# Convolution operands scaled by 1/rms from the third chunk on, and four taps moved from TensorE to VectorE, in a two-layer decoder trunk

## The chip, the core and the metric

The kernel runs on one core of a Trainium2 chip. Five engines work side by side, each through its own queue of instructions and in that queue's order: TensorE (PE: products), VectorE (DVE), ScalarE (ACT), GpSimd (POOL) and SyncE (SP, which here issues most of the DMAs). They wait for one another by semaphores. SBUF is the on-chip memory of 128 partitions; PSUM holds what TensorE writes. The metric is the time of one execution on the device in microseconds (us); of several runs the median is given.

## What is computed

Two decoder layers over 512 tokens of 1024 channels. Layer 0 begins with a causal Conformer convolution, the only part that the change touches:

```python
u = rms_norm(h, conv_norm_g)                       # u = h * rsqrt(mean(h*h)) * g
a = u @ w_pw1 + b_pw1                              # 1024 -> 2048
u = a[..., :1024] * sigmoid(a[..., 1024:])
u = conv(u, dw_w) + dw_b                           # 31 taps per channel, causal
u = silu(layer_norm(u, ln_g, ln_b))
h = h + u @ w_pw2 + b_pw2
```

Behind it come a SwiGLU feed-forward part, a gated per-layer embedding p, and layer 1 with differential attention. All data is float32.

## The kernel before

Activations lie with channels on partitions: `h[c]` is chunk c (0 to 7) of 128 channels by 512 tokens. A float32 product is made of three products in a rounded format: each operand is split into a rounded half (`hi`, a ScalarE cast) and a remainder (`lo`, a subtraction), and `mm3` (L165) adds lo x hi, hi x hi and hi x lo. A weight tile of 128x1024 goes through `weight` (L148): a DMA on SP into one of two raw buffers (`wraw`), a ScalarE cast into `whi`, a subtraction into `wlo` on VectorE or GpSimd. The next DMA into a raw buffer waits until both have read it, and SP's later DMAs stand behind it in the queue.

**The first matrix, w_pw1.** For chunk c there are a gate half and a value half, each 8 x 3 products into a PSUM tile `mm` (four of them exist). The operands are h times g alone (`Norm.split`, L211); the factor 1/rms of each token isn't known yet when TensorE begins. It comes from the token-major copy of x: ScalarE squares, VectorE and GpSimd make the inverse root, `spread` (L274) writes it to all partitions of a PSUM tile (`tp`), and `rows` (L246) copies it to SBUF as `rb`. When a half is done, VectorE multiplies it by `rb` (L612 for the gate, L618 for the value); ScalarE takes the sigmoid (L613); VectorE adds the value's bias and multiplies by the gate (L624 or L632; the "forming" instruction).

**The taps.** Chunks 1, 3, 5 and 6 (`PHASED`) are convolved on TensorE: the formed chunk goes to device memory and comes back ordered by token phases (`phased_in`, tile `C1`), TensorE multiplies by banded matrices that are loaded from `diag` (L462, into PSUM `sc` or `mm`), ScalarE copies the result (L470) and stores it (`po`, a DMA that ScalarE issues), SP loads it back in token order, and VectorE adds the bias and the mean row (`shift`, L482). Chunks 0, 2, 4 and 7 are convolved tap by tap (`other_taps`, L493): VectorE adds taps into PSUM (L518); 10, 11, 11 and 7 of the taps (`POOL_TAPS`) are products of ScalarE (L508) that GpSimd adds up (L509); and eight of chunk 7 (`PE_TAPS`) are products of TensorE with diagonal matrices (L412, in full float32). `BETWEEN` and `BEHIND` say at which chunk's matrix products the taps of an earlier chunk are issued.

**Statistics.** Once y of chunk 0 is there, its column mean (L558) gives `shrow`, a row that is added to all later chunks before their sums are taken; the first VectorE tap of chunks 2, 4 and 7 reads it (L541, L522). `moments` (L564) squares each y on ScalarE, and GpSimd adds sums and squares (L575, L571). For chunk 7 the order on VectorE is written out by hand: first tap, two taps, `shift` of chunk 5, 11 taps, `shift` of chunk 6, two taps, two additions. TensorE then fills its time with products for the embedding p (`factor`), transposes the sums (L671), and after the inverse root the rows with w_pw2 follow.

**Order.** Where no order is written by hand (`manual_schedule`, `issue_after`), a list scheduler places each instruction in its engine's queue. `pfeatures` (L357) loads p for layer 0 into the same two raw buffers and splits it, the remainder on GpSimd (L362).

Of the kernel before, what the change touches and what calls it, by code (L numbers as in the profile page):

```python
# [13 lines left out]
F32R = mybir.dt.float32r  # L14
# [6 lines left out]
P = 128  # L21
# [28 lines left out]
WARM = 9  # L50
ALONE = (7,)
CUTS = 2


PE_TAPS = (0, 0, 0, 0, 0, 0, 0, 8)
POOL_TAPS = (10, 0, 11, 0, 11, 0, 0, 7)


# [33 lines left out]
def trunk(ctx, tc, xT, xtok, pT, wts, diag, dww, vec, rel, onehot, lamv, out):  # L92
# [97 lines left out]
    def both(t):  # L190
        return t[:, 0], t[:, 1]
# [12 lines left out]
    class Norm:  # L204


        def __init__(self, g, acc_engine=None):
            self.g, self.u = g, []
            self.eng = acc_engine or G

        def split(self, c):  # L211
            hi, lo = both(sb([P, 2, S], f"A{c}", 1, F32R))
            split_scaled(h[c], col(self.g, c), hi, lo)
            self.u.append((hi, lo))

# [30 lines left out]
        def rows(self):  # L246

            r = sb([P, S], "rb", 1)
            last_rows[0] = A.copy(r, spread(self.dg))
            return r  # L250

    last_v = [None]
    last_pow = [None]
# [32 lines left out]
    raws = [sb([P, 1024], "wraw", 2) for _ in range(2)] + [sb([P, 1024], f"B{i}", 1) for i in (2, 3)]
    first = [tuple(sb([P, 1024], t, 4, F32R) for t in ("whi", "wlo")) for _ in range(4)]
    pieces = slice(0, HT), slice(HT, S), slice(S, 1024)
# [46 lines left out]

    with tc.manual_schedule(engines={V.engine, A.engine}):
        first_split(0, pieces[0])
        norm.split(0)
        first_split(1, pieces[0])
        norm.split(1)  # L340
        first_split(0, pieces[1])
        first_split(1, pieces[1])
        norm.split(2)
        norm.split(3)
        first_split(0, pieces[2])
        first_split(1, pieces[2])
        for c in range(4, NC):
            norm.split(c)
        first_split(2, whole)
        square(0)  # L350
        square(1)
        first_split(3, whole)
        square(2)
        square(3)
        norm.factors_of(sums_x)

    def pfeatures(layer, parts):  # L357
        for k, (hi, lo) in enumerate(parts):
            raw = sb([P, 1024], "wraw", 2)[:, :S]
            nc.sync.dma_start(raw, pT[layer, :, k * S : (k + 1) * S])  # L360
            A.copy(hi, raw)
            (G if layer == 0 else V).tensor_tensor(lo, raw, f(hi), ALU.subtract)  # L362
        return parts

    last_product = [None]
# [15 lines left out]
    accs = {}  # L381
    last_tap = [None]
    outs = {}
    shifts = []
    last_part = [None]
    outer = []
# [8 lines left out]
    def wt(c, j):  # L395
        return dwt[:, c * KW + j : c * KW + j + 1]
# [70 lines left out]
    def phased_out(c):  # L467

        o = big()
        A.copy(o, accs[c])  # L470
        d = dram.tile([P, S], F32, tag=f"po{c}", name=f"po{c}")
        outs[c] = nc.scalar.dma_start(d, o)
        both_ = sb([P, 2, S], f"B{c}", 1)
        for g in range(NPH):
            nc.sync.dma_start(
                both_[g * FG : (g + 1) * FG, 1].rearrange("p (r n) -> p r n", r=NPH),
                bass.AP(d.tensor, d.offset + g * P, [[S, FG], [FG * S, NPH], [1, P]]),
            )
        tok = "p (n r) -> p n r"

        def shift():
            V.scalar_tensor_tensor(  # L482
                both_[:, 0].rearrange(tok, r=NPH), both_[:, 1].rearrange("p (r n) -> p n r", r=NPH), col("dw_b", c),
                shrow.rearrange(tok, r=NPH), ALU.add, ALU.add,
            )
            y[c] = both_[:, 0]

        if c < NC - 3:
            shift()
        else:  # L490
            shifts.append(shift)

    def other_taps(c, behind=None):  # L493
        if c in PHASED:
            return phased_out(c)
        up, acc = ups[c], accs[c]
        alone = c in ALONE
        tap = lambda j: up[:, j : j + S]
        a, b = PE_TAPS[c], PE_TAPS[c] + POOL_TAPS[c]
        pacc = wk()  # L500
        for j in range(a, b):
            if j == a:
                with tc.issue_after(outs[5].ins) if alone else nullcontext():
                    A.activation(pacc, tap(j), AF.Identity, scale=wt(c, j), bias=col("dw_b", c))
            else:
                pr = sb([P, S], f"C{2 + j % 2}", 2)
                with tc.issue_after(outs[6 if j == b - 1 else 5].ins) if alone else nullcontext():
                    A.activation(pr, tap(j), AF.Copy, scale=wt(c, j))  # L508
                last_part[0] = G.tensor_tensor(pacc, pacc, pr, ALU.add)  # L509
        yc = sb([P, 2, S], f"B{c}", 1)  # L510
        if c == 0:
            sums["acc"] = yc[:, 1]
        yc = yc[:, 0]
        sum_ = sc() if alone else acc

        def taps(js):
            for j in js:
                V.scalar_tensor_tensor(sum_, tap(j), wt(c, j), sum_, ALU.mult, ALU.add)  # L518

        if alone:  # L520
            with tc.manual_schedule(engines={V.engine}):
                V.scalar_tensor_tensor(sum_, tap(b), wt(c, b), shrow, ALU.mult, ALU.add)  # L522
                taps(range(b + 1, b + 3))
                shifts[0]()
                moments(NC - 3)
                taps(range(b + 3, KW - 2))
                shifts[1]()
                outer.append(weight(eng=G, after=(last_part[0], None)))
                taps(range(KW - 2, KW))
                moments(NC - 2)  # L530
                outer.append(weight(eng=G, after=(last_sq[0], None)))
                V.tensor_tensor(yc, sum_, pacc, ALU.add)
                V.tensor_tensor(yc, acc, yc, ALU.add)
                y[c] = yc
                moments(c)
            return
        with tc.issue_after(behind.ins) if behind else nullcontext():
            if c == 0:
                V.tensor_scalar(sum_, tap(b), wt(c, b), None, ALU.mult)
            else:  # L540
                V.scalar_tensor_tensor(sum_, tap(b), wt(c, b), shrow, ALU.mult, ALU.add)  # L541
        taps(range(b + 1, KW))
        V.tensor_tensor(yc, sum_, pacc, ALU.add)
        y[c] = yc

# [8 lines left out]
    def moments(c):  # L554
# [21 lines left out]
        if c == NC - 2:  # L576
            add_square()

    for c in range(NC):
        wa, wg = pairs[c]  # L580
        if c == 0:
# [14 lines left out]
                    if k == 0:  # L596
                        rb = norm.rows()
        if 0 < c < NC - 1:
            late = ((first_gate, last_rows[0]),) * 2 if c == 1 else ((None, None),) * 2
            pairs.append(tuple(weight(after=i) for i in late)[::-1])  # L600
            pair_loads.append(loaded[0])
        if c == 1:
            ph = pfeatures(0, [(sb([P, S], t, 2, F32R), sb([P, S], t, 2, F32R)) for t in ("wth", "wtl")])
        if c > 0:
            pg = half(wg) if c > 1 else g1
            for k in BETWEEN[c]:
                pe_taps(k)
            pa = half(wa) if c > 1 else a1
            for k in BEHIND[c]:
                pe_taps(k)  # L610
        tg, ta = big(), big()
        V.tensor_tensor(tg, pg, rb, ALU.mult)  # L612
        gated = A.activation(tg, tg, AF.Sigmoid, bias=col("b_pw1", 8 + c))  # L613
        if c == NC - 1:

            with tc.issue_after(gated.ins):
                A.activation(powers[:, 24:32], vt[:, :8], AF.Silu)
        scaled = V.tensor_tensor(ta, pa, rb, ALU.mult)  # L618
        if c == 0:
            first_gate = scaled  # L620
        if c in PHASED:
            up = big()
            phases, tok = "p (r n) -> p n r", "p (n r) -> p n r"
            formed = V.scalar_tensor_tensor(  # L624
                up.rearrange(phases, r=NPH), ta.rearrange(tok, r=NPH), col("b_pw1", c),
                tg.rearrange(tok, r=NPH), ALU.add, ALU.mult,
            )
            phased_in(c, up)
        else:
            up = ups[c] = sb([P, S + PAD], "C0", 2)  # L630
            G.memset(up[:, :PAD], 0.0)
            V.scalar_tensor_tensor(up[:, PAD:], ta, col("b_pw1", c), tg, ALU.add, ALU.mult)  # L632
        for k in BETWEEN[c] + BEHIND[c]:
            other_taps(k, formed if k == 4 else None)
        if c == 1:
# [947 lines left out]
```

## Time and profile before

| | |
|---|---|
| time, median of 3 runs | 1236.92 us (1236.35 to 1238.66) |
| the profiled execution, own time | 1238.28 us |
| its span, first to last instruction | 1236.3 us |
| TensorE busy | 1224.5 us (99%) |
| VectorE, ScalarE, GpSimd busy | 880.1, 625.1, 474.3 us |
| mean granted clock of TensorE | 0.999 |

Rows of the profile name the source line (L518), the engine, the operation, the tiles written and read, and a count (x11). In a timeline a row begins with its start and its length in us; in groups, busy time and the mean of one in ns stand behind the bar, then the idle time of the engine ahead of it and what ended that. In the rows by stage the engines are in the order PE, PEld (weight loads of TensorE), DVE, ACT, POOL, and then the granted clock, the share of DMA and GB/s. The chain of waits follows the work that ended last back through what released it. TensorE's products overlap: one takes 0.39 us, the next begins sooner.

### The profile page before, as it was taken

To read this page: it belongs to the slowest core of one execution; us is meant where nothing else is said; L and a number is where in the kernel's file an instruction comes from. 1 tells how busy PE (TensorE), PEld (TensorE's weight loads), DVE (VectorE), ACT (ScalarE), POOL (GpSimd) and SP (SyncE) were. 2 spreads that over 40 slices of the span, in tenths; PEclk is the share of its full clock that TensorE was granted. 3 is DMA by queue.
4 is the path that set the end of the run, shared out by engine and by line. 5 is a ranking of instruction groups with operands and counts; after the bars stand their busy time and mean duration, and the time that the engine had idled before them with its cause. 6 is when DMAs were issued, how large, how long until landed. Compare 5 with 4: busy or idle time off the path is not lost.

```text
span 1236.3 us, 18296 instructions
## 1 busy us (share of the span) xinstructions
PE 1224.5 (99%) x7011; PEld 1072.4 (87%) x7011; DVE 880.1 (71%) x1251; ACT 625.1 (51%) x1099; POOL 474.3 (38%) x355
## 2 busy tenths in 40 slices
PE   9999999999999999999999999999999999999998
PEld 7888688888998899888788888888889998999887
DVE  5889866975895479547767776747966884588545
ACT  6563464533553255434657777735534552455432
POOL 0594813024670464133436636131026640562220
PEclk9999999999999999999999999999999999999999
DMA  8664323333333322334423321142243333233331
GB/s 328 224 209 144 106 68 110 93 106 119 93 96 119 102 86 73 116 105 153 125 85 105 99 86 53 56 150 85 90 132 90 100 120 108 80 103 86 105 99 69
DMA packets 50019, 138.44 MB, mean 112 GB/s; under 512 B 5731, under 2 KB 10851, under 8 KB 49932
## 3 DMA queue, kind: packets, MB, share of 16 engines
q1 hardware_dynamic: 47664, 133.71, 35.1%
q10 hardware_dynamic: 2268, 3.57, 1.0%
q8 instruction: 55, 0.90, 0.3%
q14 instruction: 32, 0.26, 0.1%
HBM read 130.94 MB, written 6.31 MB: 111 GB/s over the span
## 4 chain that ended last, share of the span: by engine, by line
PE 84%; DVE 7%; DMA 4%; issue 3%; ACT 1%; POOL 1%; SPq 0%; ACTq 0%; DVEq 0%; POOLq 0%
PE mm L167 26%; PE mm L168 26%; PE mm L169 26%; DMA wraw<-in_wts 2%; DVE sc L518 2%; PE mm L1282 1%; DVE wlo L162 1%; PE sc L1242 1%; PE tp L1269 1%; PE sc L1239 1%; PE sc L462 1%; DMA B<-po 1%; DVE wlo L863 1%; POOL wk L509 0%; PE tp L1190 0%
## 5 line engine op out<-in xcount | busy, mean ns | idle before, releaser
L160 ACT CAST whi<-wraw 128x1024 fp32r<-128x1024 f32 (+1 forms) x139 | 141.3, 1026 | 233.4 <-PE mm L169 108.5
L167 PE MATMUL mm<-A,wlo 128*128 128x512 f32 (+1 forms) x540 | 209.7, 388 | 0.7 <-ACT A L201 0.6
L162 DVE TENSOR_TENSOR wlo<-wraw,whi 128x1024 fp32r<-128x1024 f32 (+1 forms) x132 | 167.6, 1276 | 59.7 <-ACT whi L160 59.2
L168 PE MATMUL mm<-A,whi 128*128 128x512 f32 (+1 forms) x540 | 208.6, 386 | 0.0
L169 PE MATMUL mm<-A,whi 128*128 128x512 f32 (+1 forms) x540 | 206.6, 387 | 0.1
L167 PE MATMUL mm<-B,wlo 128*128 128x512 f32 x352 | 137.0, 389 | 0.0
L168 PE MATMUL mm<-B,whi 128*128 128x512 f32 x352 | 137.0, 389 | 0.0
L224 POOL TENSOR_TENSOR acc<-acc,wk 128x512 f32<-128x512 f32 x35 | 60.9, 1741 | 195.3 <-ACT wk L223 170.8
L169 PE MATMUL mm<-B,whi 128*128 128x512 f32 x352 | 135.6, 389 | 0.0
L168 PE MATMUL mm<-C,whi 128*128 128x256 f32 x448 | 126.8, 283 | 0.0
L169 PE MATMUL mm<-C,whi 128*128 128x256 f32 x448 | 126.8, 283 | 0.0
L167 PE MATMUL mm<-C,wlo 128*128 128x256 f32 x448 | 126.8, 283 | 0.0
L863 DVE TENSOR_TENSOR wlo<-A,whi 128x1024 fp32r<-128x1024 f32 x60 | 106.7, 1789 | 20.0 <-ACT whi L862 20.0
L167 PEld LDWEIGHTS mm<-A,wlo 128*128 128x128 f32 x540 | 101.5, 188 | 22.0 <-ACT A L201 1.0
L169 PEld LDWEIGHTS mm<-A,whi 128*128 128x128 f32 x540 | 101.5, 188 | 21.3 <-DVE A L202 0.8
L168 PEld LDWEIGHTS mm<-A,whi 128*128 128x128 f32 x540 | 101.6, 188 | 20.1
L862 ACT CAST whi<-A 128x1024 fp32r<-128x1024 f32 x60 | 63.1, 1051 | 55.7 <-PE mm L169 44.7
L872 POOL TENSOR_TENSOR A<-wraw 128x512 f32<-128x512 f32 x16 | 24.7, 1541 | 170.8 <-DMA wraw<-in_wts 155.3
L168 PEld LDWEIGHTS mm<-C,whi 128*128 128x128 f32 x448 | 86.0, 192 | 0.2
L167 PEld LDWEIGHTS mm<-C,wlo 128*128 128x128 f32 x448 | 86.0, 192 | 0.2
L169 PEld LDWEIGHTS mm<-C,whi 128*128 128x128 f32 x448 | 86.0, 192 | 0.0
L872 POOL TENSOR_TENSOR A<-A 128x512 f32<-128x512 f32 x16 | 24.7, 1546 | 159.0 <-DMA A<-in_wts 156.5
(354 smaller groups left out, 3083.5 us busy)
## 6 DMA issues: line engine op xcount, KB each, us to landing
wraw<-in_wts SPq DMA_DIRECT2D x159, 512.0 KB, 3.6
A<-in_wts SPq DMA_DIRECT2D x32, 512.0 KB, 3.7
wraw<-in_wts SPq DMA_DIRECT2D x16, 384.0 KB, 3.1
D<-in_diag SPq DMA_DIRECT2D x18, 256.0 KB, 5.2
C<-in_diag SPq DMA_DIRECT2D x16, 256.0 KB, 5.2
h<-in_xT SPq DMA_DIRECT2D x8, 256.0 KB, 4.1
B<-in_xtok SPq DMA_DIRECT2D x4, 512.0 KB, 7.6
rest<-h SPq DMA_DIRECT2D x8, 256.0 KB, 2.0
```

The lines of the kernel that those rows point to most:

```text
L160: A.copy(hi[:, cut], raw[:, cut])
L162: eng.tensor_tensor(lo[:, cut], raw[:, cut], f(hi[:, cut]), ALU.subtract)
L167: T.matmul(acc, al, bh, start=first, stop=False, **kw)
L168: T.matmul(acc, ah, bh, start=False, stop=False, **kw)
L169: return T.matmul(acc, ah, bl, start=False, stop=last, **kw)
L224: self.last = self.eng.tensor_tensor(self.acc, self.acc, sq, ALU.add)
L462: last_tap[0] = T.matmul(acc[:, g * P : (g + 1) * P], w, ups[c][:, g, LEAD - m : LEAD - m + P], start=(m == 0), stop=(m == LAGS - 1),)
L518: V.scalar_tensor_tensor(sum_, tap(j), wt(c, j), sum_, ALU.mult, ALU.add)
L862: A.copy(hi, src)
L863: V.tensor_tensor(lo, src, f(hi), ALU.subtract)
L872: G.tensor_tensor(s[:, 0], r1[:, 0], r1[:, 1], ALU.add)
L1239: first = T.matmul(acc[:, :n], qs[c][:, i, cut], ks[c][:, i, 0:n], start=True, stop=False)
```

## The change

Up to chunk 1 the products use h times g as before, but these operands now lie in tiles that are needed only later (`early_home`: tiles of B, D, wth, wtl and C1). `scale_again` then makes a second set: for each of the 8 chunks VectorE multiplies h by g and by the spread row in PSUM, ScalarE rounds, and the remainder is a subtraction on VectorE, or on GpSimd for chunks 2, 4 and 6. It is one uninterrupted run on VectorE; the multiplications and forming of chunk 0 and 1 that stand behind it wait for its end. From chunk 2 on the products use this set: the multiplications by `rb` go, the sigmoid and the forming instruction read PSUM. The two halves of chunk 2 are interleaved, chunk by chunk of the operand.

Weight remainders of one half of chunk 2 and one of chunk 3 go to GpSimd. p is loaded one chunk later, and its remainders come behind GpSimd's last sum for chunk 0. Phased taps are copied and stored right after they are issued, and their shift stands behind eight taps of the next chunk. Four of the eight taps of chunk 7 go from TensorE to VectorE. Between the two shifts of the tail VectorE then has 15 taps.

The core of the diff:

```diff
-PE_TAPS = (0, 0, 0, 0, 0, 0, 0, 8)
+LO_ON_POOL = (2, 4, 6)
+PE_TAPS = (0, 0, 0, 0, 0, 0, 0, 4)
...
-            last_rows[0] = A.copy(r, spread(self.dg))
+            self.spread = spread(self.dg)
+            last_rows[0] = A.copy(r, self.spread)
             return r
+
+        def scale_again(self):
+
+            u, late = [], []
+            with tc.manual_schedule(engines={V.engine, A.engine}):
+                for c in range(NC):
+                    t = wk()
+                    V.scalar_tensor_tensor(t, h[c], col(self.g, c), self.spread, ALU.mult, ALU.mult)
+                    if late:
+                        V.tensor_tensor(*late.pop(), ALU.subtract)
+                    hi, lo = both(sb([P, 2, S], f"A{c}", 1, F32R))
+                    self.last_hi = A.copy(hi, t)
+                    if c in LO_ON_POOL:
+                        self.pool_lo = G.tensor_tensor(lo, t, f(hi), ALU.subtract)
+                    else:
+                        late.append((lo, t, f(hi)))
+                    u.append((hi, lo))
+                self.scaled = V.tensor_tensor(*late.pop(), ALU.subtract)
+            return u
...
-            (G if layer == 0 else V).tensor_tensor(lo, raw, f(hi), ALU.subtract)
+            with tc.issue_after(last_part[0].ins) if layer == 0 else nullcontext():
+                (G if layer == 0 else V).tensor_tensor(lo, raw, f(hi), ALU.subtract)
...
-        taps(range(b + 1, KW))
+        some = taps(range(b + 1, b + 8))
+        if c - 1 in back:
+            with tc.issue_after(some.ins):
+                back[c - 1]()
+        taps(range(b + 8, KW))
...
-            late = ((first_gate, last_rows[0]),) * 2 if c == 1 else ((None, None),) * 2
-            pairs.append(tuple(weight(after=i) for i in late)[::-1])
+            late = {1: ((None, None, V), (None, last_rows[0], G)), 2: ((norm.pool_lo, norm.last_hi, G), (formed, None, V))}
+            pairs.append(tuple(weight(after=i[:2], eng=i[2]) for i in late.get(c, ((None, None, V),) * 2))[::-1])
...
-        if c == 1:
+        if c == 2:
             ph = pfeatures(0, [(sb([P, S], t, 2, F32R), sb([P, S], t, 2, F32R)) for t in ("wth", "wtl")])
-        if c > 0:
+        if c == 2:
+            norm.u = scaled_u
+            pg, pa = mm(), mm()
+            for k in range(NC):
+                mm3(pg, wpart(wg, k), norm.u[k], k == 0, k == NC - 1)
+                mm3(pa, wpart(wa, k), norm.u[k], k == 0, k == NC - 1)
+        elif c > 0:
             pg = half(wg) if c > 1 else g1
             for k in BETWEEN[c]:
                 pe_taps(k)
+                if k in PHASED:
+                    phased_out(k)
...
-        V.tensor_tensor(tg, pg, rb, ALU.mult)
-        gated = A.activation(tg, tg, AF.Sigmoid, bias=col("b_pw1", 8 + c))
+        ta = big() if c < 2 else pa
+        behind_scaled = lambda: tc.issue_after(norm.scaled.ins) if c < 2 and scaled_u else nullcontext()
+        if c < 2:
+            with behind_scaled():
+                V.tensor_tensor(tg, pg, rb, ALU.mult)
+        gated = A.activation(tg, tg if c < 2 else pg, AF.Sigmoid, bias=col("b_pw1", 8 + c))
```

How the queues stand, in three places. First VectorE, from the point where the inverse rms is there (L612 and L666 multiply the gate half of chunk 0 by `rb`). Before:

```order
L264 TENSOR_TENSOR wk_187<-ident_65,r_42_185 128x512
L612 TENSOR_TENSOR big_299<-mm_194,rb_273 128x512
L618 TENSOR_TENSOR big_300<-mm_195,rb_273 128x512
L612 TENSOR_TENSOR big_332<-mm_244,rb_273 128x512
L162 TENSOR_TENSOR wlo_309<-wraw_307,whi_308 128x1024
L162 TENSOR_TENSOR wlo_315<-wraw_313,whi_314 128x1024
L632 SCALAR_TENSOR_TENSOR C_54_304<-big_300,vec_63,big_299 128x512
```

Now (L261 is the product with the spread row `tp`, L263 the remainder into the new operand tile A):

```order
L163 TENSOR_TENSOR wlo_358<-wraw_356,whi_357 128x1024
L666 TENSOR_TENSOR big_305<-mm_200,rb_279 128x512
L674 TENSOR_TENSOR big_306<-mm_201,rb_279 128x512
L261 SCALAR_TENSOR_TENSOR wk_312<-h_6_75,vec_63,tp_280 128x512
L261 SCALAR_TENSOR_TENSOR wk_316<-h_7_76,vec_63,tp_280 128x512
L263 TENSOR_TENSOR A_61_314<-wk_312,A_61_314 128x512
L261 SCALAR_TENSOR_TENSOR wk_321<-h_8_77,vec_63,tp_280 128x512
L263 TENSOR_TENSOR A_63_319<-wk_316,A_63_319 128x512
```

The run of scaling stands between the multiplications of chunk 0 and its forming; those of chunk 1 come after it. Second GpSimd, at the sums of chunk 0 (`wk`, L509 and L545) and the remainders of p (`wth` and `wtl`, from the raw buffers). Before:

```order
L509 TENSOR_TENSOR wk_347<-wk_347,C_74_352 128x512
L362 TENSOR_TENSOR wth_320<-wraw_323,wth_319 128x512
L509 TENSOR_TENSOR wk_347<-wk_347,C_75_355 128x512
L362 TENSOR_TENSOR wtl_322<-wraw_327,wtl_321 128x512
L509 TENSOR_TENSOR wk_347<-wk_347,C_76_358 128x512
```

Now, from the last scaled part to the remainders of p:

```order
L267 TENSOR_TENSOR A_73_344<-wk_341,A_73_344 128x512
L163 TENSOR_TENSOR wlo_445<-wraw_443,whi_444 128x1024
L545 TENSOR_TENSOR wk_384<-wk_384,C_89_386 128x512
L545 TENSOR_TENSOR wk_384<-wk_384,C_90_389 128x512
L545 TENSOR_TENSOR wk_384<-wk_384,C_91_392 128x512
L545 TENSOR_TENSOR wk_384<-wk_384,C_92_395 128x512
L545 TENSOR_TENSOR wk_384<-wk_384,C_93_398 128x512
L545 TENSOR_TENSOR wk_384<-wk_384,C_94_401 128x512
L545 TENSOR_TENSOR wk_384<-wk_384,C_95_404 128x512
L545 TENSOR_TENSOR wk_384<-wk_384,C_96_407 128x512
L545 TENSOR_TENSOR wk_384<-wk_384,C_97_410 128x512
L395 TENSOR_TENSOR wth_456<-wraw_459,wth_455 128x512
```

`wlo_445` is the remainder of chunk 3's gate weights; the remainders of p moved behind all nine sums. The gate weights of chunk 4 are loaded into the raw buffer that `wraw_459` leaves. Third VectorE, from the last sum of chunk 4 (y into B) to y of chunk 7. Before:

```order
L543 TENSOR_TENSOR B_177_918<-sc_835,wk_886 128x512
L618 TENSOR_TENSOR big_1180<-mm_1103,rb_273 128x512
L632 SCALAR_TENSOR_TENSOR C_210_1185<-big_1180,vec_63,big_1179 128x512
L522 SCALAR_TENSOR_TENSOR sc_1301<-C_210_1185,C_31_133,shrow_190 128x512
L518 SCALAR_TENSOR_TENSOR sc_1301<-C_210_1185,C_31_133,sc_1301 128x512 x2
L482 SCALAR_TENSOR_TENSOR B_212_1192<-B_212_1192,vec_63,shrow_190 128x512
L518 SCALAR_TENSOR_TENSOR sc_1301<-C_210_1185,C_31_133,sc_1301 128x512 x11
L482 SCALAR_TENSOR_TENSOR B_214_1201<-B_214_1201,vec_63,shrow_190 128x512
```

Now:

```order
L584 TENSOR_TENSOR B_195_954<-sc_884,wk_922 128x512
L690 SCALAR_TENSOR_TENSOR C_228_1225<-mm_1146,vec_63,big_1222 128x512
L559 SCALAR_TENSOR_TENSOR sc_1326<-C_228_1225,C_31_133,shrow_196 128x512
L554 SCALAR_TENSOR_TENSOR sc_1326<-C_228_1225,C_31_133,sc_1326 128x512 x2
L516 SCALAR_TENSOR_TENSOR B_219_1141<-B_219_1141,vec_63,shrow_196 128x512
L554 SCALAR_TENSOR_TENSOR sc_1326<-C_228_1225,C_31_133,sc_1326 128x512 x15
L516 SCALAR_TENSOR_TENSOR B_230_1232<-B_230_1232,vec_63,shrow_196 128x512
```

The multiplication ahead of the forming is gone, and 15 taps stand between the shifts of chunks 5 and 6.

More of the change, by code (lines that the diff above doesn't have):

```diff
@@ L208, in __init__, with split @@
             self.g, self.u = g, []
+            self.pool_lo = self.last_hi = None
             self.eng = acc_engine or G
-        def split(self, c):
-            hi, lo = both(sb([P, 2, S], f"A{c}", 1, F32R))
+        def split(self, c, home=None):
+            hi, lo = home or both(sb([P, 2, S], f"A{c}", 1, F32R))
             split_scaled(h[c], col(self.g, c), hi, lo)
@@ L285, in trunk, with early_home @@
     wnext[0] = 4
+    def early_home(c):
+        if c < 2:
+            return both(sb([P, 2, S], f"B{c}", 1, F32R))
+        if c < 5:
+            return tuple(sb([P, S], f"D{2 * (c - 2) + i}", 1, F32R) for i in range(2))
+        tags = ("wth", "wtl") if c < 7 else ("C1", "C1")
+        return tuple(sb([P, S], t, 2, F32R) for t in tags)
     raws = [sb([P, 1024], "wraw", 2) for _ in range(2)] + [sb([P, 1024], f"B{i}", 1) for i in (2, 3)]
@@ L337, in trunk @@
         first_split(0, pieces[0])
-        norm.split(0)
+        norm.split(0, early_home(0))
         first_split(1, pieces[0])
-        norm.split(1)
+        norm.split(1, early_home(1))
         first_split(0, pieces[1])
         first_split(1, pieces[1])
-        norm.split(2)
-        norm.split(3)
+        norm.split(2, early_home(2))
+        norm.split(3, early_home(3))
         first_split(0, pieces[2])
@@ L347, in trunk @@
         for c in range(4, NC):
-            norm.split(c)
+            norm.split(c, early_home(c))
         first_split(2, whole)
@@ L383, in trunk @@
     outs = {}
+    back = {}
     shifts = []
@@ L488, in phased_out @@
         if c < NC - 3:
-            shift()
+            back[c] = shift
         else:
@@ L494, in other_taps @@
         if c in PHASED:
-            return phased_out(c)
+            if c not in outs:
+                phased_out(c)
+            return
         up, acc = ups[c], accs[c]
@@ L517, in taps @@
             for j in js:
-                V.scalar_tensor_tensor(sum_, tap(j), wt(c, j), sum_, ALU.mult, ALU.add)
+                last = V.scalar_tensor_tensor(sum_, tap(j), wt(c, j), sum_, ALU.mult, ALU.add)
+            return last
         if alone:
@@ L577, in moments @@
             add_square()
+    scaled_u = formed = None
     for c in range(NC):
@@ L610, in trunk @@
                 pe_taps(k)
-        tg, ta = big(), big()
-        V.tensor_tensor(tg, pg, rb, ALU.mult)
-        gated = A.activation(tg, tg, AF.Sigmoid, bias=col("b_pw1", 8 + c))
+        tg = big()
+        ta = big() if c < 2 else pa
+        behind_scaled = lambda: tc.issue_after(norm.scaled.ins) if c < 2 and scaled_u else nullcontext()
+        if c < 2:
+            with behind_scaled():
+                V.tensor_tensor(tg, pg, rb, ALU.mult)
+        gated = A.activation(tg, tg if c < 2 else pg, AF.Sigmoid, bias=col("b_pw1", 8 + c))
         if c == NC - 1:
@@ L617, in trunk @@
                 A.activation(powers[:, 24:32], vt[:, :8], AF.Silu)
-        scaled = V.tensor_tensor(ta, pa, rb, ALU.mult)
+        if c < 2:
+            with behind_scaled():
+                scaled = V.tensor_tensor(ta, pa, rb, ALU.mult)
         if c == 0:
             first_gate = scaled
+            scaled_u = norm.scale_again()
         if c in PHASED:
@@ L631, in trunk @@
             G.memset(up[:, :PAD], 0.0)
-            V.scalar_tensor_tensor(up[:, PAD:], ta, col("b_pw1", c), tg, ALU.add, ALU.mult)
+            with behind_scaled():
+                V.scalar_tensor_tensor(up[:, PAD:], ta, col("b_pw1", c), tg, ALU.add, ALU.mult)
         for k in BETWEEN[c] + BEHIND[c]:
```

## Prediction

> **What bounds the kernel now.** I read the page first, then busy time by stage, then who waited for whom, then the chain. The page says that TensorE is full:
>
> ```profile
> span 1236.3 us, 18296 instructions
> PE 1224.5 (99%) x7011; PEld 1072.4 (87%) x7011; DVE 880.1 (71%) x1251; ACT 625.1 (51%) x1099; POOL 474.3 (38%) x355
> ```
>
> The share hides where the 12 us without TensorE lie. Busy time by stage (stretch, its length, then each engine) shows three stretches: convolution with VectorE at 53 of 56 us, the step from convolution to layer norm, and the rest:
>
> ```profile
> 68.07:124.50 56.43, 55.22 (x331) 48.46 (x330) 53.41 (x61) 24.93 (x35) 37.72 (x26) 1.00 0.58 176
> 145.70:155.24 9.54, 8.24 (x35) 5.38 (x34) 6.39 (x14) 5.63 (x12) 7.72 (x5) 1.00 0.15 55
> 155.24:1236.30 1081.06, 1075.40 (x6233) 949.08 (x6231) 752.93 (x1090) 542.00 (x977) 386.08 (x284) 1.00 0.33 99
> ```
>
> TensorE's waits between 29 and 156 us are all near the end of the convolution:
>
> ```profile
> PE tp L726 <- ACT wk L723: 1.3, 1, 1.3
> PE sc L462 <- DMA B<-po: 0.9, 1, 0.9
> PE sc L671 <- POOL acc L575: 0.9, 1, 0.9
> PE mm L671 <- POOL B L571: 0.6, 1, 0.6
> PE mm L462 <- DMA C<-pi: 0.3, 1, 0.3
> ```
>
> The chain of waits there (start, length, what) does not run through TensorE at all:
>
> ```profile
> 107.16 8.28 PE sc L462 x72
> ...
> 121.90 0.59 ACT big L470
> 122.51 5.00 DMA po<-big
> 127.52 0.33 SPq L475
> ...
> 128.84 2.09 DMA B<-po
> 130.96 1.98 DVE B L482
> ...
> 144.98 0.69 DVE B L533
> 145.67 1.80 DVE r L693 x3
> ...
> 155.40 0.23 PE mm L775
> ```
>
> TensorE ends the phased taps of chunk 5, ScalarE copies them, they go to memory and back (121.9 to 130.96), and VectorE then runs the taps of chunk 7 between the two shifts until y of chunk 7 stands at 144.98 + 0.69 = 145.67. From there to the first product with w_pw2 it is fixed work, 9.6 us. The instructions behind that point stand in the same order in both programs but for a few neighbours. So the change is worth what it moves the 145.67, and nothing else.
>
> **The change, part by part.**
>
> *First two chunks.* The same instructions on other tiles: nothing. TensorE reaches chunk 2 at 29.87, chunk 4 at 59.70, and ends the last half of chunk 7 at 120.52 + 0.39 = 120.91; eight taps of chunk 7 cost 7.0 us:
>
> ```profile
> 29.87 0.39 PE L167 MATMUL mm<-A,wlo 128*128 128x512 f32 x1
> ...
> 59.70 0.39 PE L167 MATMUL mm<-A,wlo 128*128 128x512 f32 x1
> ...
> 120.52 0.39 PE L169 MATMUL mm<-A,whi 128*128 128x512 f32 x1
> ...
> L412 PE MATMUL mm<-C,D 128*128 128x512 f32 x16 | 7.0, 592 | 0.0
> ```
>
> Products follow each other by 0.23 us (the chain's last row).
>
> *VectorE's run of scaling.* The rows for its prices, and for those below:
>
> ```profile
> 12.15 2.76 DVE L202 SCALAR_TENSOR_TENSOR A<-h,vec,A 128x512 fp32r<-128x512 f32 x4
> ...
> 25.88 0.69 DVE L612 TENSOR_TENSOR big<-mm,rb 128x512 f32<-128x512 f32 x1 [1.84 <-ACT rb L249]
> ...
> 68.07 1.42 DVE L541 SCALAR_TENSOR_TENSOR sc<-C,C,shrow 128x512 f32<-128x512 f32 x1
> ...
> 132.86 8.65 DVE L518 SCALAR_TENSOR_TENSOR sc<-C,C,sc 128x512 f32<-128x512 f32 x11
> ...
> L162 DVE TENSOR_TENSOR wlo<-wraw,whi 128x1024 fp32r<-128x1024 f32 x13 | 18.6, 1435 | 2.8 <-ACT whi L160 2.8
> L624 DVE SCALAR_TENSOR_TENSOR big<-big,vec,big 128x512 f32<-128x512 f32 x4 | 7.5, 1872 | 0.2
> L612 DVE TENSOR_TENSOR big<-mm,rb 128x512 f32<-128x512 f32 x8 | 5.5, 685 | 2.1 <-ACT rb L249 1.8 <-PE mm L169 0.3
> L482 DVE SCALAR_TENSOR_TENSOR B<-B,vec,shrow 128x512 f32<-128x512 f32 x2 | 3.3, 1638 | 1.9 <-DMA B<-po 1.9
> ```
>
> It adds 8 products with the spread row and 5 subtractions, at 2.76/4 = 0.69 each 9.0 us. No row has a product with one operand in PSUM and one in SBUF of this kind; between the 0.69 and a tap's 8.65/11 = 0.79 it is 9.0 to 9.8; that a spread row in PSUM is read faster, no row excludes. It removes 12 multiplications by rb (chunks 2 to 7) at 0.685, 8.2 us; two weight remainders go to GpSimd, 2.9 us; four taps come, 4 x 0.79 = 3.15. Together VectorE has about 1 us more, but it has it elsewhere: at the start, and in the tail.
>
> Does TensorE wait for the scaled operands? The first product is there at 25.88 + 3 x 0.69 = 28.0; ScalarE has a weight cast, a table load and a sigmoid first (rows below: 1.04, 1.28, 0.72) and ends the first rounded half at 25.9 + 3.04 + 0.6 = 29.5. TensorE asks at 29.87, and then for a new chunk each 6 x 0.23 = 1.38 us, where VectorE needs 1.38, and 0.69 for the three that GpSimd ends. The run ends near 37, and its last part is asked for at 40.0. Hidden, with 0.4 us to spare at the start.
>
> *GpSimd's queue, and with it the weights of chunk 4.* Here I see the price.
>
> ```profile
> 39.14 10.41 POOL L509 TENSOR_TENSOR wk<-wk,C 128x512 f32<-128x512 f32 x6
> ...
> 128.12 3.98 POOL L509 TENSOR_TENSOR wk<-wk,C 128x512 f32<-128x512 f32 x3 [0.47 <-ACT C L508]
> ...
> L162 POOL TENSOR_TENSOR wlo<-wraw,whi 128x1024 fp32r<-128x1024 f32 x1 | 2.4, 2350 | 0.0
> L362 POOL TENSOR_TENSOR wth<-wraw,wth 128x512 fp32r<-128x512 f32 x1 | 1.3, 1315 | 0.0
> ...
> L160 ACT CAST whi<-wraw 128x1024 fp32r<-128x1024 f32 x16 | 16.5, 1044 | 7.4 <-DMA wraw<-in_wts 6.6 <-ACT big L470 0.5 <-PE mm L169 0.3
> ...
> wraw<-in_wts SPq DMA_DIRECT2D x159, 512.0 KB, 3.6
> ...
> po<-big ACTq DMA_DIRECT2D x4, 256.0 KB, 2.9
> ```
>
> GpSimd now has the gate weights of chunk 3 behind the scaled parts: last scaled cast near 36.5, weight cast 1.04, remainder 2.35, so 39.9; TensorE asks at 29.87 + 48 x 0.23 = 40.9. Then come nine partial sums of chunk 0 in one row, and behind them the remainders of p, which before stood between the sums. The raw buffer of p is the one that the gate weights of chunk 4 are loaded into, on SP, and SP's queue waits with it. A sum takes 3.98/3 = 1.33 to 10.41/6 = 1.74; I take the middle, since VectorE mostly runs taps beside them: 40.0 + 9 x 1.53 = 53.8, + 1.31 = 55.1, + 3.6 for the load = 58.7, + 1.04 cast = 59.7, + 1.44 remainder on VectorE = 61.2. TensorE is there at 59.70: a new wait of 1.5 us, with ends of 0 (sums at 1.33, remainder below the mean) and 3.3 (sums at 1.74).
>
> *VectorE up to chunk 7.* The column sum of chunk 0 stands behind 32 products of chunk 4: 61.2 + 32 x 0.23 = 68.6, then a matmul, a copy and a VectorE step by the like rows (0.39, 0.59, 0.69): 70.3, where the run of 68.07 began before, 2.2 later. Of the 56.43 us from there, seven multiplications go (7 x 0.685 = 4.8 us) and 1.9 us of waits for reloaded chunks, which are now stored right behind their taps. The forming instructions (mean 1.87) now read one operand in PSUM; that may save up to 4.6 us in all, if they come down to a tap's price, or nothing. So y of chunk 4 is done at 70.3 + 49.7 = 120.0 or earlier. TensorE ends the last half of chunk 7 at 120.91 - 0.94 (the wait for chunk 5's reload order goes) + 1.5 = 121.5. VectorE is there first, and chunk 7 is formed at once; before it was formed 4 us behind TensorE.
>
> *The tail.* Chunk 5's taps end at 107.16 + 8.28 - 0.94 + 1.5 = 116.0. ScalarE now has copy, sigmoid and a table load ahead of the store:
>
> ```profile
> 118.38 0.72 ACT L613 ACTIVATE big<-big,vec 128x512 f32<-128x512 f32 x1 [6.93 <-DVE big L612]
> 119.12 1.28 ACT L617 ACT_TABLE_LOAD   x1
> ```
>
> 116.0 + 0.59 + 0.72 + 1.28 = 118.6. The store took 5.0 in the chain and 2.9 in the median; I take the middle, 122.6. Reload as before, 130.96 - 127.52 = 3.44: 126.0. VectorE itself has formed chunk 7 and done three taps by 121.5 + 0.8 + 1.1 + 1.6 = 125.0 (the first tap, with two operands in SBUF, between 0.79 and 1.42), so the reload sets it. From the shift to y took 145.67 - 130.96 = 14.71 with 11 taps between; now 15, + 3.15, and a reduction of 0.6 that stands ahead of the last addition: 126.0 + 14.71 + 3.15 + 0.6 = 144.5. That is 1.2 us earlier. TensorE's four taps, 3.5 us, lie where it waits anyway (0.9 and 0.6): they buy only a longer wait there. With all bounds low the reload is there at 123.4 and y at 141.9, 3.8 earlier; with all high, 1.6 later.
>
> The profiled execution took 1238.28, 2.0 more than its span and 1.4 more than the median of 1236.92. 1238.28 - 1.2 is 1237.1 for an execution like it; for the median 1235.7, its own range 1233.1 to 1238.5. About 0.2%, 2.5 us, is what a measurement of this kernel can tell from no change.
>
> **The rivals.** *The weights of chunk 4 come in time*, 1233.1: sums at 1.33, and VectorE with the reload early. For it: three of GpSimd's sums at 128 did run so. Against it: six did not, beside weight remainders like those here.
>
> *GpSimd falls behind*, slower. VectorE's steps with two operands in SBUF and GpSimd's sums slow each other (1.42 for L541 against a tap's 0.79; 1.74 against 1.33). The remainder for chunk 3 slips by 1.1 us, past the 40.9, and nine sums take 1.74: 41.0 + 15.6 + 1.31 + 3.6 + 1.04 + 1.44 = 64.0, a wait of 4.3, and the store takes its 5.0: 2.6 us later, 1239.5. It decides once the ninth sum ends later than 56. For it: 1.74 at 39.14. Against it: this stretch has fewer such steps.
>
> *TensorE does set the end*, so that four taps give their 3.5: 1233.4. Against it stands the chain above, with no product between 121 and 151.
>
> *A clock that drops.* TensorE ends its fill at 121.5 + 8.3 + 3.5 + 30 x 0.23 = 140.2 (phased row, half the tap row, products) and waits for y of chunk 6, 3.6 us ahead of 144.5, and GpSimd's sum behind it, until near 142.3: 2.1 us where the row has 0.9. In the rows above the granted clock stays 1.00, and no wait is over 1.3. If a wait that long halves the clock for a few us, the transposes and products in the 9.5 us behind it cost about 1.5 more, 1237.2.
> [...]
>
> **How the numbers follow.** Forecast 0.44, weights in time 0.28, GpSimd behind 0.17, TensorE sets the end 0.05, clock 0.06. Faster by over 2.5 us (under 1234.4): the second and fourth, less a little, 0.32; slower (over 1239.4): 0.17; within: 0.51. The range runs from below the fast cases, 1232.6 (the run of scaling may cost less than the rows say), to 1239.2, into the slow case.
>
> **What would show it.** Right: a TensorE wait of about 1.5 us at chunk 4 for a weight remainder; chunk 7 formed right behind its last product, near 121.5; chunk 5's shift near 126 behind a DMA; a longer TensorE wait before the transposes; y of chunk 7 near 144.5. Wrong: no wait at chunk 4, or waits at chunks 2 and 3; VectorE late at chunk 7; y moved by more than 2.5 us; or a different time behind an unmoved y.

## The result, and the profile after

The changed kernel takes 1234.98 us in the median of 15 runs (1234.02 to 1237.35), the kernel before 1236.97 (1235.96 to 1238.98): ratio 0.9983, 95% interval 0.9975 to 0.9991. A second comparison, on another occasion, gave 1237.09 against 1238.24, ratio 0.9991 (0.9982 to 1.0000), an interval that ends at no change. The gain is 1.2 to 2.0 us, under the 2.5 us that the forecast called the least that can be told from nothing; 1.2 was forecast, with 1235.7 for the median.

The profiled execution took 1234.18, with this head of its page:

```profile
span 1232.3 us, 18295 instructions
PE 1221.3 (99%) x7003; PEld 1071.1 (87%) x7003; DVE 876.0 (71%) x1254; ACT 629.4 (51%) x1107; POOL 483.5 (39%) x360
```

Its span is 4.0 us under that of before, twice the difference of the medians: the execution profiled before lay 1.3 above its median, this one 0.8 below. So a second execution of each was profiled (below). Busy time by stage, for VectorE's row up to the sum of chunk 4, the step to layer norm, and the rest:

```profile
73.98:119.62 45.64, 45.64 (x276) 40.55 (x275) 43.93 (x53) 22.62 (x31) 34.16 (x25) 1.00 0.64 211
141.73:150.95 9.22, 8.13 (x33) 5.36 (x33) 5.92 (x13) 4.67 (x10) 7.35 (x5) 1.00 0.21 57
150.95:1232.30 1081.35, 1075.54 (x6233) 949.07 (x6231) 752.88 (x1090) 541.32 (x977) 388.49 (x284) 1.00 0.31 99
```

The last two together are as long as before (1090.57 us, where 9.54 and 1081.06 make 1090.60), with the same 6233 products: in this execution all that changed lies ahead of y of chunk 7. TensorE's waits between 25 and 160 us:

```profile
PE mm L168 <- DVE wlo L163: 1.2, 1, 1.2
PE tp L784 <- ACT wk L781: 1.0, 1, 1.0
PE sc L729 <- POOL acc L616: 0.6, 1, 0.6
PE mm L729 <- POOL B L612: 0.6, 1, 0.6
PE sc L729 <- DVE B L570: 0.2, 1, 0.2
```

The first is the new wait at chunk 4, at 60.60, of 1.17 us. None stands at chunk 2 or 3, where the scaled operands begin. The chain of waits through the end of the convolution:

```profile
107.28 8.05 PE sc L496 x72
...
115.97 4.63 DMA po<-big
120.62 0.33 SPq L509
...
121.94 2.21 DMA B<-po
124.33 1.13 DVE B L516
...
137.12 1.14 DVE B L516
```

It runs through chunk 5's round trip as before, but by a hair only. VectorE's own row reaches the shift (L516) at the same moment:

```profile
118.93 0.69 DVE L584 TENSOR_TENSOR B<-sc,wk 128x512 f32<-128x512 f32 x1
120.88 0.75 DVE L690 SCALAR_TENSOR_TENSOR C<-mm,vec,big 128x512 f32<-128x512 f32 x1 [1.26 <-PE mm L170]
121.67 1.17 DVE L559 SCALAR_TENSOR_TENSOR sc<-C,C,shrow 128x512 f32<-128x512 f32 x1
122.87 1.55 DVE L554 SCALAR_TENSOR_TENSOR sc<-C,C,sc 128x512 f32<-128x512 f32 x2
124.33 1.13 DVE L516 SCALAR_TENSOR_TENSOR B<-B,vec,shrow 128x512 f32<-128x512 f32 x1
...
141.05 0.68 DVE L570 TENSOR_TENSOR B<-mm,B 128x512 f32<-128x512 f32 x1
```

Chunk 7 is formed right behind its last product (VectorE had waited 1.26 us for it), and from 120.88 to 141.73 VectorE works without a gap. y of chunk 7 stands at 141.73, against 145.67 before.

### The profile page after: what moved, and what is told of

Same layout as the page of the kernel before. It is cut to its first block, busy times and chain, and to the rows that moved or that the text cites. A ratio compares the mean times of both kernels' runs of the same rounds, so it can differ in the third digit from the quotient of the medians.

```text
span 1232.3 us, 18295 instructions
## 1 busy us (share of the span) xinstructions
PE 1221.3 (99%) x7003; PEld 1071.1 (87%) x7003; DVE 876.0 (71%) x1254; ACT 629.4 (51%) x1107; POOL 483.5 (39%) x360
## 4 chain that ended last, share of the span: by engine, by line
PE 92%; DVE 3%; DMA 2%; ACT 1%; issue 1%; POOL 0%; SPq 0%; ACTq 0%; DVEq 0%; POOLq 0%
PE mm L168 28%; PE mm L169 28%; PE mm L170 28%; PE mm L1340 1%; PE sc L496 1%; DVE sc L554 1%; DMA wraw<-in_wts 1%; PE sc L1300 1%; PE tp L1327 1%; PE sc L1297 1%; PE tp L1248 1%; DMA h<-in_xT 0%; DVE wlo L163 0%; DMA po<-big 0%; PE tp L1370 0%
## 5 line engine op out<-in xcount | busy, mean ns | idle before, releaser
L163 DVE TENSOR_TENSOR wlo<-wraw,whi 128x1024 fp32r<-128x1024 f32 (+1 forms) x130 | 164.3, 1269 | 62.7 <-ACT whi L161 62.3
L168 PE MATMUL mm<-A,wlo 128*128 128x512 f32 (+1 forms) x524 | 203.1, 388 | 1.3 <-DVE wlo L163 1.2
L169 PE MATMUL mm<-A,whi 128*128 128x512 f32 (+1 forms) x524 | 202.4, 386 | 0.0
L170 PE MATMUL mm<-A,whi 128*128 128x512 f32 (+1 forms) x524 | 198.9, 386 | 0.0
L168 PE MATMUL mm<-B,wlo 128*128 128x512 f32 x356 | 139.0, 390 | 0.0
L169 PE MATMUL mm<-B,whi 128*128 128x512 f32 x356 | 138.8, 390 | 0.0
L170 PE MATMUL mm<-B,whi 128*128 128x512 f32 x356 | 137.4, 389 | 0.0
L169 PE MATMUL mm<-C,whi 128*128 128x256 f32 (+1 forms) x450 | 127.6, 283 | 0.0
L170 PE MATMUL mm<-C,whi 128*128 128x256 f32 (+1 forms) x450 | 127.5, 283 | 0.0
L168 PE MATMUL mm<-C,wlo 128*128 128x256 f32 (+1 forms) x450 | 127.5, 283 | 0.0
L168 PEld LDWEIGHTS mm<-A,wlo 128*128 128x128 f32 x524 | 98.4, 188 | 21.9 <-DVE wlo L163 1.6
L170 PEld LDWEIGHTS mm<-A,whi 128*128 128x128 f32 x524 | 98.4, 188 | 20.0
L169 PEld LDWEIGHTS mm<-A,whi 128*128 128x128 f32 x524 | 98.5, 188 | 19.6
L920 ACT CAST whi<-A 128x1024 fp32r<-128x1024 f32 x60 | 62.8, 1047 | 56.0 <-PE mm L170 45.1
```

Of the source, the lines that this page charges most:

```text
L163: eng.tensor_tensor(lo[:, cut], raw[:, cut], f(hi[:, cut]), ALU.subtract)
L168: T.matmul(acc, al, bh, start=first, stop=False, **kw)
L169: T.matmul(acc, ah, bh, start=False, stop=False, **kw)
L170: return T.matmul(acc, ah, bl, start=False, stop=last, **kw)
L920: A.copy(hi, src)
```

## The experiments

**Second executions of both kernels.** Nothing edited.

> The kernel before, unchanged, for a second profiled execution. In the two profiled executions y of chunk 7 stood at 145.67 us before and 141.73 us after, 3.9 us apart, and the spans are 4.0 apart, but the medians of 15 runs only 2.0. If the first 156 us vary from one execution to the next (the round trip of chunk 5 through memory, 8.45 us from its store to the shift, is the candidate), y of chunk 7 should now stand 1 to 2 us earlier, near 144.2. If they do not vary, y stands within 0.3 us of 145.67 and the difference between profile and median lies behind 156 us.

> The changed kernel, unchanged, for a second profiled execution and a second comparison. Expected ratio 0.998 to 0.999 of the kernel before. y of chunk 7 within 0.5 us of 141.73 if VectorE's unbroken row behind the last product of chunk 7 (120.77 us) sets it; later by 0.5 to 1.5 us, behind a wait of the shift of chunk 5 for a DMA, if the round trip through memory sets it in most executions.

The chain of the second execution of before (the last row is y's final addition):

```profile
121.66 3.83 DMA po<-big
...
128.85 1.90 DVE B L482
...
143.78 0.69 DVE B L533
```

The store of chunk 5 took 3.83 us where it took 5.00, and y stood at 144.47 in place of 145.67. What follows y is 1090.6 us in both. The second execution of after had y at 144.11, 2.4 later than the first:

```profile
126.73 1.15 DVE L516 SCALAR_TENSOR_TENSOR B<-B,vec,shrow 128x512 f32<-128x512 f32 x1 [0.60 <-DMA B<-po]
...
143.43 0.68 DVE L570 TENSOR_TENSOR B<-mm,B 128x512 f32<-128x512 f32 x1
```

Its chunk 2 began 0.35 later, its wait at chunk 4 was 0.6 longer, the first tap of chunk 7 took 1.82 where it took 1.17, its store took 5.42, and VectorE waited 0.60 for the reload. So y varied by 1.2 us between the two executions of before and by 2.4 between those of after. The mean of the two y is 145.07 before and 142.92 after, 2.15 apart; the spans, 1235.7 and 1234.0 in the mean, are 1.7 apart, and the medians 1.2 and 2.0. The second execution of after shows something else: TensorE's wait ahead of the transposes was long, and the granted clock (the column of 0.82 and 0.50, third from the right) fell behind it.

```profile
PE sc L729 <- POOL acc L616: 1.9, 1, 1.9
PE mm L168 <- DVE wlo L163: 1.8, 1, 1.8
```

```profile
142.00:143.00 1.00, 0.66 (x4) 0.42 (x4) 0.87 (x3) 0.00 (x0) 1.00 (x1) 0.82 0.00 0
143.00:144.00 1.00, 0.73 (x4) 0.72 (x4) 1.00 (x2) 0.00 (x0) 1.00 (x2) 0.50 0.00 0
144.00:145.00 1.00, 1.00 (x6) 0.84 (x5) 0.69 (x2) 0.63 (x1) 1.00 (x1) 0.50 0.00 0
```

What follows y took 1091.6 us here, 1.0 more than in the other three. The first product with w_pw2 came 9.68 us behind y, where it came 9.22 behind it in the first execution of after (141.73 to 150.95 above):

```profile
153.79 0.39 PE L833 MATMUL mm<-A,wlo 128*128 128x512 f32 x1
```

**The scaled operands without the tap move.**

```diff
-PE_TAPS = (0, 0, 0, 0, 0, 0, 0, 4)
+PE_TAPS = (0, 0, 0, 0, 0, 0, 0, 8)
```

> The changed kernel with eight taps of chunk 7 on TensorE again, as before; the scaled operands stay. Theory (each part needs the other): VectorE has 4 x 0.79 = 3.15 us less behind 120.77, so y of chunk 7 stands at about 138.6 to 139.0; but TensorE's row from 120.61 to its last fill product, which ended at 139.07 without a gap, gets 4 x 0.875 = 3.5 us longer and ends at 142.6, and the four groups of transposes behind it end 2.0 us later than after: 2.0 us slower than after, about the time of before, with no wait of TensorE at the transposes. Rival (the forecast on record: TensorE's four taps lie where it waits anyway, and the round trip of chunk 5 sets the end): TensorE has the room, and the time is that of after less 1 to 3 us, 1232 to 1234.

Measured: 1237.70, ratio 0.9999 to before (0.9990 to 1.0008). VectorE's last addition and the step behind it, then TensorE's transposes:

```profile
141.34 0.69 DVE L570 TENSOR_TENSOR B<-mm,B 128x512 f32<-128x512 f32 x1
144.28 0.69 DVE L751 TENSOR_REDUCE r<-sc 128x4 f32<-128x512 f32 x1 [2.24 <-PE sc L729]
```

```profile
143.41 0.39 PE L170 MATMUL mm<-wtl,whi 128*128 128x512 f32 x1
143.64 0.60 PE L729 MATMUL sc<-ident,acc 128*128 128x128 f32 x4
```

y is done at 142.03 and VectorE then waits 2.24 us for TensorE, which goes from its last fill product to the transposes without a gap: with eight taps TensorE is what is late. The scaled operands, with the changes of order that came with them, alone move nothing that can be measured. That four taps do better than eight behind them rests on this trace: the two ratios, 0.9999 here and 0.9991 (0.9982 to 1.0000) with four on the same occasion, have intervals that overlap. My figure for y (138.6 to 139.0) was wrong: chunk 7 was formed 1.1 later here, the two shifts took 1.78 and 1.90 where they took 1.13 and 1.14, and VectorE waited 1.05 for the two reloads.

**The tap move without the scaled operands.** The kernel before with its `PE_TAPS` at 4.

> The kernel before with four taps of chunk 7 on TensorE and four more on VectorE, and nothing else of the change. Theory (VectorE and the round trip set the end of before): y of chunk 7 stands 3.1 us later (4 x 0.79), TensorE waits 3.5 + 3.1 us longer ahead of the transposes, 3 us slower, about 1240. Rival (TensorE sets the end of before): 3.5 us of TensorE's work gone, 2 to 3 us faster, about 1234.

Measured: 1241.01, ratio 1.0023 (1.0014 to 1.0032), 2.8 us slower. TensorE's longest wait, and VectorE's last addition:

```profile
PE sc L671 <- POOL acc L575: 5.9, 1, 5.9
```

```profile
147.42 0.68 DVE L533 TENSOR_TENSOR B<-mm,B 128x512 f32<-128x512 f32 x1
```

y at 148.10 is 3.0 behind the mean of the two executions of before, for 4 x 0.79 = 3.15. In the kernel before VectorE and the round trip set the end, and TensorE's taps are worth nothing. With four taps, then, the rest of the change is worth 3.9 us: 1241.01 without it, 1237.09 with it on the same occasion. No run separates the scaled operands from the changes of order among that rest.

**Three places that the forecast named.** The remainders of p (`p_early`):

```diff
-            with tc.issue_after(last_part[0].ins) if layer == 0 else nullcontext():
+            with nullcontext():
```

> The changed kernel without the order that puts the two remainders of p behind the nine partial sums of chunk 0 on GpSimd; they stand between the sums again, as before. Theory (the sums hold the raw buffer of p, and it the gate weights of chunk 4): the wait of TensorE at chunk 4 (1.17, 1.81 and 1.80 us in the three profiled executions with that order) is under 0.2, the copy of chunk 5 and the last product of chunk 7 come 1.2 to 1.8 us earlier, and y of chunk 7 with them: 1.2 to 1.8 us faster than the changed kernel, 0.9985 to 0.999 of it. Rival (something else is late next): the wait goes but VectorE, whose row of chunk 4 ended only 1.26 and 0.61 us ahead of the last product of chunk 7, then sets the forming of chunk 7, and no more than 0.6 us is won. Second rival: the wait stays because the load itself is slow.

Measured: 1236.60, ratio 0.9985 (0.9976 to 0.9993), the level of the changed kernel. Its two longest waits:

```profile
PE sc L729 <- POOL acc L616: 2.0, 1, 2.0
PE sc L496 <- DMA C<-pi: 1.3, 1, 1.3
```

The wait at chunk 4 is gone, so the chain from GpSimd's sums through p's raw buffer to those weights is shown. But TensorE now comes to the taps of chunk 3 before they are back from memory (1.3 us), and VectorE forms chunk 7 at 121.28, 0.8 behind TensorE, since its row of chunk 4 ends only then. Something else was next in line, as the first rival said.

The store ahead of the sigmoid (`store_first`):

```diff
-        gated = A.activation(tg, tg if c < 2 else pg, AF.Sigmoid, ...)
+        with tc.issue_after(outs[5].ins) if c == NC - 1 else nullcontext():
+            gated = A.activation(tg, tg if c < 2 else pg, AF.Sigmoid, ...)
```

> The changed kernel with the store of chunk 5 ahead of the sigmoid of chunk 7 and the table load on ScalarE's row. On record was that the two cost the store 0.72 + 1.28 = 2.0 us. The traces have the store 0.03 us behind the end of the copy in one execution and 0.84 and 0.69 us behind it in two, each time 0.1 to 0.23 us into the table load. Theory (a store is issued while the engine still computes, and is held at most by the start of the table load): the store is always 0.03 us behind the copy, 0 to 0.8 us earlier, and y moves by 0 to 0.6, which the times hardly tell from nothing. Rival (the record's): 2 us earlier, up to 2 us faster.

Measured: 1236.63, ratio 0.9985 (0.9976 to 0.9994): no 2 us. ScalarE in the changed kernel, where the store (L506) stands behind sigmoid and table load in the queue, first and second execution:

```profile
115.35 0.59 ACT L504 COPY big<-sc 128x512 f32<-128x512 f32 x1 [5.29 <-PE sc L496]
115.84 0.70 ACT L667 ACTIVATE big<-mm,vec 128x512 f32<-128x512 f32 x1
115.97 0.35 ACTq L506 DMA_DIRECT2D po<-big  x1
116.55 1.28 ACT L671 ACT_TABLE_LOAD   x1
```

```profile
116.41 0.59 ACT L504 COPY big<-sc 128x512 f32<-128x512 f32 x1 [4.66 <-PE sc L496]
116.89 0.70 ACT L667 ACTIVATE big<-mm,vec 128x512 f32<-128x512 f32 x1
117.61 1.28 ACT L671 ACT_TABLE_LOAD   x1
117.84 0.35 ACTq L506 DMA_DIRECT2D po<-big  x1
```

In the first the store goes out 0.03 us behind the end of the copy, while the engine is in the sigmoid; in the second 0.84 behind it, during the table load.

The shift of chunk 5 behind six taps (`shift_later`):

```diff
-                taps(range(b + 1, b + 3))
+                taps(range(b + 1, b + 6))
```

> The changed kernel with the shift of chunk 5 behind six taps of chunk 7 instead of three on VectorE, 2.4 us later in its row. Theory (VectorE's own row sets y of chunk 7, and the round trip only now and then by up to 0.6 us): no wait of VectorE for the reload, y of chunk 7 0 to 0.6 us earlier, same time. Rival (the forecast on record: the reload of chunk 5 sets the end, VectorE is ready 1 us ahead of it): y 1 us or more earlier, 1 us faster.

Measured: 1236.08, ratio 0.9984 (0.9975 to 0.9993), and VectorE did not wait for the reload. The time stayed; the round trip costs little in the changed kernel.

**The three together.**

> The changed kernel with the three edits together: remainders of p between the sums, store of chunk 5 ahead of the sigmoid, shift of chunk 5 three taps later. If the wait at chunk 4 is all that stands ahead of the row of VectorE behind the last product of chunk 7: 1.2 to 2.2 us faster than the changed kernel, 0.997 of the kernel before. If VectorE's row of chunk 4 or TensorE's row of fill products takes over: within 0.6 us of the changed kernel.

Measured: 1236.93, ratio 0.9990 (0.9981 to 0.9999). The three do not add up: TensorE waited 1.4 us for chunk 3 and 2.0 at the transposes, with the clock at 0.50 behind that.

**TensorE kept busy in its wait.**

```diff
+    with tc.issue_after(last_product[0].ins):
+        for _ in range(6):
+            last_product[0] = T.matmul(sums["mean"], ones_r, ph[0][0], start=True, stop=True)
```

> The changed kernel with six products more on TensorE (1.4 us, their result is overwritten by the next product into the same bank) between the last product of the fill and the first transposes, where TensorE waits for GpSimd. Five of the seven profiled executions with four taps on TensorE show the granted clock at 0.50 for 3.4 us (6.8 in one) from 0.4 to 1.2 us behind that wait of 0.8 to 5.9 us; in none of three with eight taps is it below 1.00 there. Theory (the wait that four fewer taps leave on TensorE sets the clock back): no clock under 1.00 between 138 and 150 us, fewer executions with a mean clock of 0.998 or less (11 of 26 runs of the changed kernel so far), and the median 0.3 to 1 us lower although work was added. Rival (the clock falls for another reason, or the fall costs nothing since VectorE sets y there): same time or 0.3 us slower, clock unchanged.

Measured: 1236.31, ratio 0.9993 (0.9984 to 1.0002). Between 138 and 150 us the clock stays at 1.00 (in this execution it fell to 0.50 behind the wait of 1.84 us at chunk 4), and one execution in 11 has a mean clock of 0.998 or less, against 11 in 26 of the changed kernel on the two earlier occasions. That speaks for the wait as what sets the clock back. The counts alone don't show it: the changed kernel was not run on this occasion, and with eight taps, where the trace has no wait ahead of the first transposes, 4 executions in 11 were that low. The time did not fall. From y to the first product with w_pw2 took 9.58 us, 0.1 less than with the low clock in the second execution of after. (The sentence on record says that all the falls came behind the wait; with the taps alone the clock fell inside the wait of 5.9 us.)

**Six taps.** `PE_TAPS` at 6, and the same with the edit of p.

> The changed kernel with six taps of chunk 7 on TensorE, between the eight of before and the four of the change. Theory (VectorE's row from the last product of chunk 7 to y, 20.9 us without a gap, and TensorE's row from there to the transposes, which ends 0.6 to 1.9 us ahead of what it waits for, are the two ends of a balance): y of chunk 7 1.6 us earlier than with four, TensorE's last fill product 1.75 us later and no wait of more than 0.3 us ahead of the first transposes, no clock under 1.00 there; 0.5 to 1.2 us faster than the changed kernel. Rival (the time is a straight line between eight taps, level with before, and four): 0.5 to 1 us slower than the changed kernel.

> Six taps on TensorE, and the remainders of p between the partial sums of chunk 0 again. With the remainders there alone TensorE's wait at chunk 4 (1.2 to 2.5 us) went and a wait of 1.3 us for the reordered chunk 3 took its place, while at the end a wait of 1.95 us and the clock at 0.50 behind it stood. Theory: with six taps that end is balanced, so what p gives (0 to 1.2 us) is no longer lost there: 0.8 to 2 us faster than the changed kernel. Rival (the wait for chunk 3 takes it all): level with six taps alone.

Measured: 1235.76, ratio 0.9981 (0.9972 to 0.9990), and 1234.92, ratio 0.9979 (0.9970 to 0.9987), each to 1237.93 for before. All of TensorE's waits between 25 and 160 us, with six taps alone:

```profile
PE mm L168 <- DVE wlo L163: 1.7, 1, 1.7
PE tp L784 <- ACT wk L781: 1.6, 1, 1.6
```

and with both edits:

```profile
PE tp L784 <- ACT wk L781: 1.4, 1, 1.4
PE sc L496 <- DMA C<-pi: 0.9, 1, 0.9
PE mm L729 <- POOL B L612: 0.4, 1, 0.4
```

The wait ahead of the first transposes is gone in both (the 0.4 stands ahead of the second group), and one execution in 22 has a clock of 0.998 or less. y stands at 141.22 and 141.58. Both versions beat the kernel before. They have the lowest ratios of all runs, but their intervals overlap with those of the changed kernel, so that they beat it too is not shown.

## Why the prediction held, step by step

**The scaling run is hidden: right.** TensorE began chunk 2 at 29.38 without a wait, and GpSimd ended the gate weights of chunk 3 at 37.25 + 2.64 = 39.89, where 39.9 was forecast.

**The new wait at chunk 4: right.** GpSimd in the changed kernel, with the nine sums and p behind them:

```profile
37.25 2.64 POOL L163 TENSOR_TENSOR wlo<-wraw,whi 128x1024 fp32r<-128x1024 f32 x1 [1.03 <-ACT whi L161]
39.86 13.73 POOL L545 TENSOR_TENSOR wk<-wk,C 128x512 f32<-128x512 f32 x9
53.53 1.29 POOL L395 TENSOR_TENSOR wth<-wraw,wth 128x512 fp32r<-128x512 f32 x1
```

The ninth sum ended at 53.59 (forecast 53.8), and the wait was 1.17 here and 1.72 to 2.53 in the other six executions with that order (forecast 1.5, ends 0 and 3.3). The rivals "weights in time" and "GpSimd behind" both fell. The first would hardly have given its 1233.1: in the run with the p edit alone, which had no wait at chunk 4, chunk 3's reload and VectorE's row took its place.

**VectorE is there before chunk 7: right, by two errors that cancel.** Its run with `shrow` began at 73.98, not 70.3, since weight remainders ahead of it waited for their casts (2.87 us before the one at 71.35). It then took 45.64 us, not 49.7: the three forming instructions in it (0.75, 1.17 and 1.14 us) took 3.06 us, where before they took 1.75, 1.87 and 3.27, 6.89 in all. That is 3.8 us of the saving of up to 4.6 that was left open. (The 1.87 of the forecast is the mean of L624 alone; those of L632 had a mean of 1.22.) Chunk 4's sum was done at 119.62, within the 120.0.

**The tail: one term wrong, and the sum near in one execution of two.** "ScalarE now has copy, sigmoid and a table load ahead of the store" failed: the 2.0 us were 0.02 or 0.03 in six of the eight executions with that order and 0.7 to 0.8 in two. The row of instructions told the order, not the time: in the six the store waited for the copy's end and not for the work that stands between. The taps of chunk 5 also ended 0.7 earlier than forecast. With the store at 115.97 in place of 118.6, its 4.63 us (3.95 taken) and the reload, the shift stood at 124.33, not 126.0. The row from there to y took 17.40, not 18.5, mainly since the shift took 1.13 where 1.98 was carried over. So this execution has y at 141.73 where 144.5 was forecast. By the prediction's own signs it spoke against it: y moved by 3.9 us, over the 2.5 that were to show it wrong, and TensorE's wait ahead of the first transposes (0.60) was not longer than before (0.87). The second execution has these signs (y at 144.11, a wait of 1.91, the shift at 126.73 behind a DMA), in part by luck: its store left at 117.84, held by 0.84 us and not by 2.0, and took 5.42 us, not 3.95. A y from one execution is uncertain by 1 to 2 us; the forecast was worked from a before at 145.67, the later of two. In the means of two, y moved by 2.15 us where 1.2 was forecast.

**The four taps: half wrong.** That they buy only a longer wait holds for the kernel before, where they alone cost 2.8 us. It does not hold behind the scaled operands: there eight taps make TensorE late (VectorE waits 2.24 us for it), so that by this trace the move is needed for the gain. "TensorE sets the end" had 0.05 and is true of the scaled half of the change by itself. The two parts, level and 2.8 slower when alone, give 1.2 to 2.0 together.

**The clock: the rival was underrated.** It had 0.06, my estimate, for a wait of 2.1 us. That such a wait halves the clock for a few us was assumed there, since no row of before shows it; the runs show 0.50 for 3.4 us. Waits of 1.9 to 2.0 ahead of the transposes came in three of the seven profiled executions with four taps and nothing to fill the wait, and in these, as in two others, the clock fell to 0.50. It did not cost the 1.5 us there: from y to the first product with w_pw2 took 9.68 to 9.69 us in the three with the long wait, 9.21 and 9.22 in the two without a low clock there, so about 0.5. With the wait filled the time did not fall. Over all executions the account stays open: in the changed kernel those with a mean clock of 0.998 or less took 1.2 and 1.4 us more in the mean than the others of their occasion, but a late y may bring both a longer wait and a longer time, and spells at chunk 4 (below) may be among them.

## What to carry to other kernels

Work that moves from one engine to another is worth what the later of the two rows then shows, so a change of two parts is priced as a whole: one part can make room that only the other uses. When a wait is taken away, the next thing in line has to be named with its own time; without the wait at chunk 4, a reload and VectorE's row stood right behind it. And where two profiled executions of one kernel differ by 1 to 2 us in the stretch that matters, a second profile is worth more than a finer sum over one.

## What the hardware showed that was not expected

**The clock can fall after waits of about 2 us.** With the remainders of p behind the sums and the store moved, TensorE waited 2.53 us at chunk 4, until 61.66, and the clock was low from 62.8 to 66.2:

```profile
63.00:66.00 3.00, 3.00 (x8) 2.32 (x7) 2.87 (x3) 2.18 (x5) 0.00 (x0) 0.50 0.88 343
```

Each low spell lasted 3.4 us, with the taps alone 6.8. At chunk 4 it cost 1.6 us: from chunk 2's start to the copy of chunk 5, less the wait, this execution took 118.02 - 29.05 - 2.53 = 86.44 us, the first of the changed kernel 115.35 - 29.38 - 1.17 = 84.80. The one other execution with a spell there (the run with the wait filled) took 86.41 by the same sum. Waits of 1.72 to 1.96 at chunk 4 were followed by a spell in one of five executions, those of 1.9 to 2.0 ahead of the transposes in three of three, and waits of 0.8, 0.6 and 0.2 within 3 us of each other in one, so the single wait's length does not decide it alone. What else does, no run here shows.

**A store can leave while the engine whose queue it stands in is still computing.** In six of eight executions it left 0.02 or 0.03 us behind the copy that it waits for, during the sigmoid that stands ahead of it in the queue; in two it left 0.69 and 0.84 us behind it, during the table load. What holds it then stays open.
